# Where the modulation weights' dot products run beside three FFNs, and when a third FFN forms its sums of blocks

## The chip, the cores and the metric

The kernel runs on one core of a Trainium2 chip. The metric is the device time of one execution in microseconds (us); lower is better. PE is TensorE's matmul queue, DVE is VectorE, ACT is ScalarE, POOL is GpSimd, and SP is the queue from which nearly all transfers are issued.

## The reference, cut to what matters

Two layers run over 640 tokens: 128 context tokens and 512 latent tokens. Each layer has an FFN, a mixing of four head groups, and a second FFN. Each of these is normed, modulated and gated by vectors computed from the condition:

```
mod = silu(cond) @ w_mod + b_mod            # 9 vectors of 1024 for each layer and each condition
sh1, sc1, g1, sh2, sc2, g2, sh3, sc3, g3 = split(mod, 9)
x = x + 0.5 * g1 * swiglu(modulate(rmsnorm(x, nw0), sh1, sc1), w_in0, w_out0)
x = x + g2 * mixing(modulate(rmsnorm(x, nw1), sh2, sc2))
x = x + 0.5 * g3 * swiglu(modulate(rmsnorm(x, nw2), sh3, sc3), w_in1, w_out1)
swiglu(h) = (silu(h @ w_gate) * (h @ w_up)) @ w_out      # hidden width 2816
```

All of it is float32.

## The kernel before, in words

The activations lie transposed, 128 of the 1024 channels to a tile `x` and the 640 tokens in two groups of 320. A float32 product is done as three passes in a rounded format (fp32r): an operand is split into `hi`, a copy that ACT rounds, and `lo`, the difference that DVE takes (`split` and `wsplit`; the subtraction is line 61). So each weight tile of 128 x 1024 numbers goes from a load (`raw`, three buffers) to `hi` on ACT, to `lo` on DVE, and only then to PE; `hi` and `lo` have three buffers each.

Four FFNs run one after the other: the first (layer 0, function `ffn`), the second (layer 0 behind the mixing), the third (layer 1 before the mixing) and the fourth (layer 1 behind it); the last three are `ffn7`. The hidden width has 22 tiles. The first `ndir` of them (2, 12 and 2 in the second, third and fourth FFN) are direct: `direct` does for each token group the gate product and the up product, 24 matmuls each, so 96 in a tile, then `sg` (silu times up) and the split of the result into `gh` and `gl`. The other tiles are "quads" (`quad`): gate and up over both token groups as seven products of 12 matmuls in place of eight, as in Strassen's scheme. They need sums of weight blocks (`sa`, `sb`, made by DVE from `raw`) and sums of activation blocks (`T`, made by `sums(j)` from the normed values `nv` in `V`: four sums and three splits into `th` and `tl` for each j). A quad's products are taken in the order B21, B11, T3, T2, T4, then, between the products of the next quad, T1 and B22. After 5, 10, 15 and 19 tiles `down` multiplies by the output weights, eight column blocks, and adds to `x` with the gate (`accumulate`).

The modulation vectors of later norms are computed meanwhile on DVE. `modulation` is a generator: for each of 72 tiles of 128 outputs a layer it loads 128 x 1024 weights (`wm`, two buffers) and does two dot products with the condition (`modpiece`, the line 271, tile `wmj`), one for each condition; each call of `next` does one such piece. `some(rate)` adds a rate to a credit and calls `next` for each whole unit. The rates of an FFN are three: for each token group of a direct tile, for each column block of `down`, and for each quad. What is left is done before the last part. With `PIN`, a piece is pinned behind everything that was written before it on DVE.

For all the rest a planner sets each engine's order from what is written: it takes what is ready by its own costs, in the order of priority, and gives out buffers; an engine then does its instructions strictly in that order. So where a piece is written changes what the planner puts ahead of what.

Of the kernel before, what the change touches and what calls it, by code (L numbers as in the profile page):

```python
# [53 lines left out]
class Trunk:  # L54
# [486 lines left out]
    def ffn7(self, li, w, todo, ndir, rates, after_group):  # L541
        I, n = self.I, 2 * w
        pool = lambda name: self.tc.tile_pool(name=name, bufs=2, side="right", reuse_waits="tile")
        with pool("ws") as sp, pool("ffn") as mp, pool("mods") as modp, self.tmp():
            mods = self.modulation(todo, modp, bufs=MBUF, pin=PIN) if todo else iter(())
            self.G = []
            credit = [0.0]

            def some(rate):

                credit[0] += rate
                while credit[0] >= 1.0:
                    next(mods, None)
                    credit[0] -= 1.0

            def finish(q):
                for _ in q:
                    pass

            def down(ff, nk):  # L560

                G, self.G = self.G[:nk], self.G[nk:]
                for m in range(8):
                    hi, lo = self.wload(I["ffnoutA"][li, w, m, :, ff * 128 : (ff + nk) * 128], nk * 128)
                    for g in range(2):
                        ps = self.mmp.tile([128, 512], F32, tag="mm", name="mm")[:, :320]
                        self.mm3(ps, [(hi[:, k * 128 : (k + 1) * 128], lo[:, k * 128 : (k + 1) * 128]) + G[k][g]
                                      for k in range(nk)])
                        self.accumulate(li, n, m, g, ps)
                    some(rates[1])  # L570

            def direct(f):

                ws = [self.wload(I["ffnin"][li, w, 2 * f + i], 1024) for i in range(2)]
                sg = mp.tile([128, 640], F32, tag="sg", name="sg", bufs=2)
                gh = self.ring("gh", 640, F32R)
                gl = self.ring("gl", 640, F32R)
                for g in range(2):
                    c = slice(320 * g, 320 * g + 320)
                    self.act(sg[:, c], self.unit(ws[0], g, shifts=False), AF.Silu)  # L580
                    self.tt(sg[:, c], self.unit(ws[1], g, shifts=False), sg[:, c], MUL)
                    self.split(gh[:, c], gl[:, c], sg[:, c])
                    some(rates[0])
                self.G.append([(gh[:, 320 * g : 320 * g + 320], gl[:, 320 * g : 320 * g + 320]) for g in range(2)])

            ends = [sum(FFN_CHUNKS[: i + 1]) for i in range(len(FFN_CHUNKS))]
            for f in range(ndir):
                direct(f)
                if f < 2:
                    self.sums(f)  # L590
                if f + 1 in ends:
                    nk = FFN_CHUNKS[ends.index(f + 1)]
                    down(f + 1 - nk, nk)
            for j in range(2):
                self.split(self.hw[0][1][:, 2 * j : 2 * j + 2, 0:320], self.hw[1][1][:, 2 * j : 2 * j + 2, 0:320], self.V[0][j])
            prev = None
            for f in range(ndir, 22):
                q = self.quad(li, w, f, sp, mp, f == 21)
                next(q)
                if prev is not None:  # L600
                    next(prev)
                next(q)
                if prev is not None:
                    finish(prev)
                    if f in ends:
                        ci = ends.index(f)
                        down(f - FFN_CHUNKS[ci], FFN_CHUNKS[ci])
                prev = q
                some(rates[2])
            finish(prev)  # L610
            for _ in mods:
                pass
            nk = FFN_CHUNKS[-1]
            ws = [self.wload(I["ffnoutB"][li, w, b], 1024) for b in range(3)]
            G = self.G
            for g in range(2):
                for m in range(8):
                    if g and m == NPOS:
                        next(done, None)
                    ps = self.mmp.tile([128, 512], F32, tag="mm", name="mm")[:, :320]  # L620
                    parts = []
                    for k in range(nk):
                        b, j = divmod(m * nk + k, 8)
                        parts.append((ws[b][0][:, j * 128 : (j + 1) * 128],
                                      ws[b][1][:, j * 128 : (j + 1) * 128]) + G[k][g])
                    self.mm3(ps, parts)
                    self.accumulate(li, n, m, g, ps)
                    if li + 1 < NL or w == 0:
                        self.square(m, g)
                if g:  # L630
                    next(done, None)
                done = after_group(g)
                next(done, None)
            next(done, None)
# [777 lines left out]
    def run(self):  # L1412
        self.setup()
        with self.tc.tile_pool(name="start", bufs=2, side="right", reuse_waits="tile") as p, self.tmp():
            nc = self.nc
            cb = self.condb_start(p)
            self.xload(self.I["xT"])
            norms = [self.norm(0, 0, g, nc.vector, True) for g in range(2)]
            scale = self.modulation([(0, 1)], p, tiles=range(4, 8), bufs=SMB, cb=cb)
            shift = self.modulation([(0, 0)], p, tiles=range(2 * SPE, 8), bufs=SMB, cb=cb)  # L1420
            for j in range(2 + SPE):
                self.modulation_start(0, 1 if j < 2 else 0, p, range(j % 2, j % 2 + 1) if j < 4 else range(j - 2, j - 1))
                for gen in (scale, scale) if j < 2 else (shift,):
                    next(gen, None)
                for g in range(2):
                    if j == SORD[g] or j == SORD[2 + g]:
                        next(norms[g], None)
            for _ in shift:
                pass
            self.shifts(0, 0)  # L1430
            ahead = [self.wload(self.I["ffnin"][0, 0, i], 1024) for i in range(2)]
            for n in norms:
                next(n, None)
        kern = self.filters(range(NL))
        todo = [[(0, i) for i in range(2, 9)], [(1, 0), (1, 1)],
                [(1, i) for i in range(2, 8)], [(1, 8)]]
        for li in range(NL):
            def n1(g):
                if g == 0:
                    self.shifts(li, 1)  # L1440
                yield from self.norm(li, 1, g)
                self.xspill(li, g)

            def n2(g):
                yield from self.norm7(li, 2, g)

            def n3(g):
                if li + 1 < NL:
                    yield from self.norm7(li + 1, 0, g)
                else:  # L1450
                    self.store(g)
                    yield

            if li == 0:
                self.ffn(li, 0, todo[0], RATES[0], n1, ahead)
            else:
                self.ffn7(li, 0, todo[2], NDIR[1], RATES[2], n1)
                self.fac.close()
            for m in range(8):
                for g in range(2):  # L1460
                    self.tap(f"x1_{li}_{m}_{g}", self.x[m][g])
            self.mix(li, kern, n2)
            for m in range(8):
                for g in range(2):
                    self.tap(f"x2_{li}_{m}_{g}", self.x[m][g])
            self.ffn7(li, 1, todo[2 * li + 1], NDIR[2 * li], RATES[2 * li + 1], n3)
        self.fac.close()
# [12 lines left out]
CGACT = True  # L1480
MBUF = 2
NPOS = 8
RATES = 2.0, (1.5, 1.0, 0.5), (2.2, 1.0, 1.0), (2.0, 1.0, 3.0)
PIN = True
WB = 3
EACT = 1
# [164 lines left out]
```

## Time and profile before

| | us |
|---|---|
| median of three runs | 2776.7 (2774.94 to 2779.11) |
| the profiled execution | 2773.57 |
| its span, first to last instruction | 2771.8 |
| PE busy in the span | 2671.7 (96%) |
| DVE busy | 1959.7 (71%) |
| ACT busy | 1030.2 (37%) |

Busy PE time is modelled at its end, since matmuls are pipelined: the start of one to the start of the next is the better measure of its pace. Of the chain of work that ended last, 89% is PE's and 5% DVE's. The second FFN begins at about 997 us of the span, the third at 1445, the fourth at 2324.

### The profile page before, as it was taken

The numbers are of one execution on the slowest core, as the hardware profiler recorded it, in microseconds if no ns is written. First come the engines' busy times: TensorE is split into PE (matmuls) and PEld (weight loads), VectorE is DVE, ScalarE is ACT, GpSimd is POOL, SyncE is SP. The second block draws the span as 40 slices with busy tenths as digits, with TensorE's granted clock in tenths as the row PEclk, the third lists the DMA queues.
The fourth block names the chain that finished last, engine by engine and source line by source line (L and its number), as shares of the span: only waits on it lengthen the run. The fifth ranks groups of instructions, "written<-read, shape, count | busy, mean of one in ns | idle before, by whom it ended". The sixth has DMA issues, their size and how long they took to land.

```text
span 2771.8 us, 45385 instructions
## 1 busy us (share of the span) xinstructions
PE 2671.7 (96%) x17870; PEld 2575.6 (93%) x17870; DVE 1959.7 (71%) x4050; ACT 1030.2 (37%) x2042; POOL 114.0 (4%) x191
## 2 busy tenths in 40 slices
PE   5999999999999989999999999998999998999999
PEld 3889999989999979999988999998999997999999
DVE  5886666665685687776667777787658578876666
ACT  3222222242455353433353223334335535343342
POOL 0000000020010020000020000002001002000000
PEclk9999999999999999999999999999999999999999
DMA  7435444431221323333213443334212132322222
GB/s 247 145 125 197 142 135 148 137 103 66 81 78 42 108 69 107 105 111 121 84 61 118 158 149 129 117 130 148 85 57 96 36 106 68 107 79 82 85 69 91
DMA packets 118389, 299.64 MB, mean 108 GB/s; under 512 B 19747, under 2 KB 42483, under 8 KB 117664
## 3 DMA queue, kind: packets, MB, share of 16 engines
q1 hardware_dynamic: 118176, 296.74, 32.6%
q8 instruction: 141, 2.31, 0.3%
q14 instruction: 72, 0.59, 0.1%
HBM read 282.49 MB, written 14.20 MB: 107 GB/s over the span
## 4 chain that ended last, share of the span: by engine, by line
PE 89%; DVE 5%; issue 2%; POOL 1%; ACT 1%; DMA 1%; SPq 0%; POOLq 0%; DVEq 0%; ACTq 0%
PE mm L88 68%; PE mx L88 10%; PE mc L88 6%; PE mb L88 3%; PE mx L93 2%; DVE lo L61 1%; POOL nsum L287 1%; DVE x L70 1%; DVE wmj L271 1%; ACT hi L76 0%; POOL nrs L120 0%; DVE hl L61 0%; DVE tl L61 0%; DVE nv L61 0%; DVE gl L61 0%
## 5 line engine op out<-in xcount | busy, mean ns | idle before, releaser
L88 PE MATMUL mm<-hh,lo 128*128 128x320 f32 (+2 forms) x2936 | 922.8, 315 | 13.0 <-DVE lo L61 13.0
L88 PE MATMUL mm<-hh,hi 128*128 128x320 f32 (+2 forms) x2936 | 927.6, 317 | 6.8 <-ACT hh L76 4.1
L88 PE MATMUL mm<-hl,hi 128*128 128x320 f32 (+2 forms) x2936 | 924.3, 315 | 2.5 <-DVE hl L61 2.1
L76 ACT CAST hi<-raw 128x1024 fp32r<-128x1024 f32 (+3 forms) x390 | 338.5, 868 | 779.0 <-PE mm L88 704.4
L88 PEld LDWEIGHTS mm<-hh,lo 128*128 128x128 f32 (+1 forms) x2936 | 558.8, 190 | 20.3 <-DVE lo L61 14.1
L88 PEld LDWEIGHTS mm<-hh,hi 128*128 128x128 f32 (+1 forms) x2936 | 557.1, 190 | 15.0 <-ACT hh L76 5.7
L88 PEld LDWEIGHTS mm<-hl,hi 128*128 128x128 f32 (+1 forms) x2936 | 556.9, 190 | 12.8 <-issue 5.1
L61 DVE TENSOR_TENSOR lo<-raw,hi 128x1024 fp32r<-128x1024 f32 (+3 forms) x390 | 387.6, 994 | 175.0 <-ACT hi L76 172.9
L88 PE MATMUL mm<-gh,hi 128*128 128x320 f32 x1408 | 438.4, 312 | 5.5 <-DVE x L70 5.5
L88 PE MATMUL mm<-gl,hi 128*128 128x320 f32 x1408 | 436.3, 311 | 0.5 <-DVE gl L61 0.3
L88 PE MATMUL mm<-gh,lo 128*128 128x320 f32 x1408 | 434.5, 309 | 0.0
L70 DVE SCALAR_TENSOR_TENSOR x<-mm,gate,x 128x128 f32<-128x128 f32 (+2 forms) x576 | 234.4, 434 | 175.2 <-PE mm L88 172.7
L271 DVE CUSTOM_DVE_ANT_0 wmj<-wm,condb 128x1024 bf16<-128x1024 f32 x264 | 321.2, 1217 | 3.0 <-ACT condb L73 1.2
L88 PEld LDWEIGHTS mm<-gh,hi 128*128 128x128 f32 x1408 | 265.1, 188 | 11.0 <-PE mm L88 9.0
L88 PEld LDWEIGHTS mm<-gl,hi 128*128 128x128 f32 x1408 | 265.3, 188 | 3.9 <-issue 1.8
L88 PEld LDWEIGHTS mm<-gh,lo 128*128 128x128 f32 x1408 | 265.0, 188 | 0.3 <-issue 0.2
L88 PE MATMUL mc<-th,lo 128*128 128x320 f32 x400 | 123.4, 309 | 0.0
L88 PE MATMUL mc<-th,hi 128*128 128x320 f32 x400 | 123.3, 308 | 0.0
L88 PE MATMUL mc<-tl,hi 128*128 128x320 f32 x400 | 123.3, 308 | 0.0
L287 POOL TENSOR_TENSOR nsum<-nsum,nsq 128x320 f32<-128x320 f32 x60 | 54.8, 914 | 1350.6 <-ACT nsq L73 945.8
L76 ACT CAST gh<-sg 128x640 fp32r<-128x640 f32 (+1 forms) x85 | 51.6, 607 | 103.7 <-DVE sg L61 103.7
L70 DVE SCALAR_TENSOR_TENSOR gu<-mm,cg,sg 128x128 f32<-128x128 f32 (+2 forms) x66 | 27.2, 435 | 76.2 <-ACT cg L76 49.0
(283 smaller groups left out, 3500.6 us busy)
## 6 DMA issues: line engine op xcount, KB each, us to landing
raw<-in_ffnin SPq DMA_DIRECT2D x176, 512.0 KB, 3.5
wm<-in_wmodT SPq DMA_DIRECT2D x132, 512.0 KB, 3.5
raw<-in_ffnoutA SPq DMA_DIRECT2D x96, 320.0 KB, 2.8
raw<-in_mixin SPq DMA_DIRECT2D x52, 512.0 KB, 3.4
raw<-in_ffnoutA SPq DMA_DIRECT2D x32, 256.0 KB, 2.6
wms<-in_wmod SPq DMA_DIRECT2D x12, 512.0 KB, 3.4
raw<-in_ffnoutB SPq DMA_DIRECT2D x12, 512.0 KB, 3.4
raw<-in_mixout SPq DMA_DIRECT2D x16, 384.0 KB, 2.9
```

What stands on the lines that cost most here:

```text
L61: self.nc.vector.tensor_tensor(out, a, b, op=op)
L70: self.nc.vector.scalar_tensor_tensor(out, a, s, b, op0=op0, op1=op1)
L76: self.nc.scalar.copy(out, in_)
L88: return self.nc.tensor.matmul(out, lhsT=lhsT, rhs=rhs, start=start, stop=stop, **k)
L93: self.nc.tensor.transpose(out, in_, self.ident[b : b + n, b : b + n])
L271: return self.nc.vector.tensor_tensor_reduce(junk, raw, cb, 1.0, 0.0, op0=MUL, op1=ADD, accum_out=out)
L287: (adder or (self.nc.vector if g and m > 5 else self.nc.gpsimd)).tensor_tensor(s, s, sq, op=ADD)
```

## The change

Two lists of numbers and one rule are changed. `todo` gives the last modulation vector (layer 1, index 8) to the third FFN in place of the fourth, which has none left. `RATES` are 0 for the direct tiles of the second and the fourth FFN. In the third FFN (`ndir` of 12, so `late` is 3) the rates have four entries: 0 beside the first direct tile, after which the list is shortened to 3.2 for each token group of a direct tile (before: 2.2), 1.0 and 1.0. And there `sums(0)` and `sums(1)` are written after the fourth and the fifth direct tile, before after the first and the second.

```
             ends = [sum(FFN_CHUNKS[: i + 1]) for i in range(len(FFN_CHUNKS))]
+            late = 0 if ndir < 6 else 3
             for f in range(ndir):
+                if late and f == 1:
+                    rates = rates[1:]
                 direct(f)
-                if f < 2:
-                    self.sums(f)
+                if 0 <= f - late < 2:
+                    self.sums(f - late)
...
         todo = [[(0, i) for i in range(2, 9)], [(1, 0), (1, 1)],
-                [(1, i) for i in range(2, 8)], [(1, 8)]]
+                [(1, i) for i in range(2, 9)], []]
...
-RATES = 2.0, (1.5, 1.0, 0.5), (2.2, 1.0, 1.0), (2.0, 1.0, 3.0)
+RATES = 2.0, (0, 1.0, 0.5), (0, 3.2, 1.0, 1.0), (0, 0, 0)
```

The third FFN has 96 pieces before and 112 after, the fourth 16 before and none after, the second 32 in both.

DVE's order at the start of the third FFN before, from the end of the first direct tile's second token group on (`raw_15012` and `raw_15018` are the gate and the up weight of the second tile, `nv` and `tl` belong to the sums of blocks):

```order
L61 TENSOR_TENSOR gl_14876<-sg_14874,gh_14875 128x320
L271 ISA wmj_14997,mod1_108<-wm_14995,condb_14931 128x1024
L271 ISA mod1_108 128x1
L61 TENSOR_TENSOR nv_14832<-nv_14832,nv_14760 128x640
L271 ISA wmj_14999,mod1_108<-wm_14995,condb_14931 128x1024
L271 ISA mod1_108 128x1
L61 TENSOR_TENSOR tl_9460<-nv_14832,th_9459 128x2x320
L61 TENSOR_TENSOR mod1_108<-mod1_108,par1_93 128x2
L61 TENSOR_TENSOR nv_14782<-nv_14782,nv_14832 128x640
L61 TENSOR_TENSOR lo_15015<-raw_15012,hi_15014 128x1024
L61 TENSOR_TENSOR tl_9460<-nv_14782,th_9459 128x2x320
L61 TENSOR_TENSOR lo_15021<-raw_15018,hi_15020 128x1024
```

The same engine and place after, from the first `sg` of the first direct tile on (`raw_14985` and `raw_14991` are now the second tile's gate and up weight, `raw_15132` the third's gate weight):

```order
L61 TENSOR_TENSOR sg_14874<-mm_14903,sg_14874 128x320
L61 TENSOR_TENSOR lo_14988<-raw_14985,hi_14987 128x1024
L61 TENSOR_TENSOR hl1_106<-nv_14832,hh1_104 128x640
L61 TENSOR_TENSOR hl1_106<-nv_14839,hh1_104 128x640
L61 TENSOR_TENSOR gl_14876<-sg_14874,gh_14875 128x320
L61 TENSOR_TENSOR nv_14760<-nv_14818,nv_14760 128x640
L61 TENSOR_TENSOR nv_14771<-nv_14825,nv_14771 128x640
L61 TENSOR_TENSOR nv_14818<-nv_14818,nv_14832 128x640
L61 TENSOR_TENSOR lo_14994<-raw_14991,hi_14993 128x1024
L61 TENSOR_TENSOR sg_14874<-mm_14957,sg_14874 128x320
L61 TENSOR_TENSOR lo_15135<-raw_15132,hi_15134 128x1024
```

The second tile's gate `lo` moved from behind the second `gl` and its pieces to directly behind the first `sg`; the sums of blocks keep much of their early place.

DVE's order in the fourth FFN before, from the second direct tile's last `gl` to the first `lo` of the first quad (`raw_24312`):

```order
L61 TENSOR_TENSOR gl_24175<-sg_24173,gh_24174 128x320
L271 ISA wmj_24293,mod1_108<-wm_24291,condb_24080 128x1024
L271 ISA mod1_108 128x1
L61 TENSOR_TENSOR tl_23252<-nv_23991,th_23251 128x2x320
L271 ISA wmj_24295,mod1_108<-wm_24291,condb_24080 128x1024
L271 ISA mod1_108 128x1
L61 TENSOR_TENSOR nv_23945<-nv_23945,nv_23991 128x640
L61 TENSOR_TENSOR mod1_108<-mod1_108,par1_93 128x2
L61 TENSOR_TENSOR hl1_106<-nv_23912,hh1_104 128x640
L61 TENSOR_TENSOR hl1_106<-nv_23923,hh1_104 128x640
L61 TENSOR_TENSOR tl_23252<-nv_23945,th_23251 128x2x320
L61 TENSOR_TENSOR lo_24319<-raw_24312,hi_24318 128x1024
```

And after (`raw_24338` and `raw_24340` are the first quad's two weights, `sg_24213` is the second direct tile's, here its first token group):

```order
L61 TENSOR_TENSOR tl_23309<-nv_23991,th_23308 128x2x320
L61 TENSOR_TENSOR lo_24210<-raw_24207,hi_24209 128x1024
L61 TENSOR_TENSOR nv_24034<-nv_24034,nv_24048 128x640
L61 TENSOR_TENSOR lo_24345<-raw_24338,hi_24344 128x1024
L61 TENSOR_TENSOR tl_23309<-nv_24034,th_23308 128x2x320
L61 TENSOR_TENSOR nv_24048<-nv_24048,nv_23980 128x640
L61 TENSOR_TENSOR sa_24342<-raw_24340,raw_24338 128x512
L61 TENSOR_TENSOR sg_24213<-mm_24242,sg_24213 128x320
L61 TENSOR_TENSOR tl_23309<-nv_24048,th_23308 128x2x320
L61 TENSOR_TENSOR gl_24215<-sg_24213,gh_24214 128x320
L61 TENSOR_TENSOR nv_24002<-nv_24002,nv_24048 128x640
L61 TENSOR_TENSOR sb_24343<-raw_24340 128x512
```

The quad's first `lo` moved from behind the second tile to ahead of its first `sg`, and the quad's sums `sa` and `sb` begin there too. The second FFN is ordered in the same way.

SP's order in the third FFN where the quads begin, before (`raw_17269` and `raw_17271` are the first quad's weights, `raw_17371` and `raw_17373` the second's):

```order
L85 DMA raw_17269<-in_ffnin 128x1024
L85 DMA wm_17120<-in_wmodT 128x1024
L85 DMA raw_17271<-in_ffnin 128x1024
L85 DMA wm_17197<-in_wmodT 128x1024
L85 DMA raw_17371<-in_ffnin 128x1024
L85 DMA raw_17373<-in_ffnin 128x1024
L85 DMA wm_17258<-in_wmodT 128x1024
L85 DMA wm_17367<-in_wmodT 128x1024
L85 DMA raw_17505<-in_ffnin 128x1024
```

And after (the first quad's are `raw_17335` and `raw_17337`, the second's `raw_17437` and `raw_17439`, the third's first `raw_17572`):

```order
L85 DMA raw_17335<-in_ffnin 128x1024
L85 DMA raw_17337<-in_ffnin 128x1024
L85 DMA wm_17170<-in_wmodT 128x1024
L85 DMA raw_17437<-in_ffnin 128x1024
L85 DMA wm_17177<-in_wmodT 128x1024
L85 DMA raw_17439<-in_ffnin 128x1024
L85 DMA wm_17253<-in_wmodT 128x1024
L85 DMA wm_17261<-in_wmodT 128x1024
L85 DMA wm_17323<-in_wmodT 128x1024
L85 DMA wm_17433<-in_wmodT 128x1024
L85 DMA raw_17572<-in_ffnin 128x1024
```

Four loads of modulation weights now stand between the second quad's weights and the third's, where there were two. Late in the second mixing the planner also orders the retention part differently, though nothing is written differently there.

## Rows read from the trace of the kernel before

**Rows 1.** The page: span and instructions; busy time, share and instructions by engine.
```profile
span 2771.8 us, 45385 instructions
PE 2671.7 (96%) x17870; PEld 2575.6 (93%) x17870; DVE 1959.7 (71%) x4050; ACT 1030.2 (37%) x2042; POOL 114.0 (4%) x191
```
**Rows 2.** Waits of PE, whole span: waiter, awaited, us in total, times, longest.
```profile
PE mb L88 <- DVE lo L61: 14.4, 2, 8.4
PE mm L88 <- DVE lo L61: 13.0, 6, 6.8
```
**Rows 3.** PE's timeline, second FFN: start, us, instruction, count, idle before and its end.
```profile
1029.16 0.64 PE L88 MATMUL mb<-hh,lo 128*128 128x320 f32 x1 [6.01 <-DVE lo L61]
...
1032.21 0.31 PE L88 MATMUL mm<-hh,hi 128*128 128x320 f32 x1
```
**Rows 4.** PE's timeline, third FFN: first slow matmul and first fast one.
```profile
1471.05 0.64 PE L88 MATMUL mm<-hh,lo 128*128 128x320 f32 x1 [6.78 <-DVE lo L61]
...
1475.96 0.31 PE L88 MATMUL mm<-hh,lo 128*128 128x320 f32 x1
```
**Rows 5.** PE's timeline, fourth FFN: first slow matmul and first fast one.
```profile
2359.01 0.63 PE L88 MATMUL mb<-hh,lo 128*128 128x320 f32 x1 [8.39 <-DVE lo L61]
...
2363.41 0.31 PE L88 MATMUL mm<-hh,lo 128*128 128x320 f32 x1
```
**Rows 6.** Windows: stretch, us, busy by engine (count), granted clock, DMA share, GB/s.
```profile
1471.00:1475.70 4.70, 4.65 (x17) 4.65 (x18) 4.67 (x6) 0.19 (x1) 0.00 (x0) 0.50 0.59 204
```
**Rows 7.** DVE's timeline, second FFN, end of the direct tiles.
```profile
1022.59 0.49 DVE L61 TENSOR_TENSOR sg<-mm,sg 128x320 f32<-128x320 f32 x1 [0.22 <-PE mm L88]
...
1027.89 1.22 DVE L61 TENSOR_TENSOR lo<-raw,hi 128x1024 fp32r<-128x1024 f32 x1
```
**Rows 8.** DVE's timeline, third FFN, first direct tile.
```profile
1457.15 0.48 DVE L61 TENSOR_TENSOR sg<-mm,sg 128x320 f32<-128x320 f32 x1
...
1469.78 1.22 DVE L61 TENSOR_TENSOR lo<-raw,hi 128x1024 fp32r<-128x1024 f32 x1
1470.92 0.81 DVE L61 TENSOR_TENSOR tl<-nv,th 128x640 fp32r<-128x640 f32 x1
```
**Rows 9.** ACT's timeline, third FFN: the second tile's gate weight.
```profile
1442.31 1.03 ACT L76 CAST hi<-raw 128x1024 fp32r<-128x1024 f32 x1
```
**Rows 10.** DVE's groups by shape: the pieces (busy us, mean ns, idle before).
```profile
L271 DVE CUSTOM_DVE_ANT_0 wmj<-wm,condb 128x1024 bf16<-128x1024 f32 x264 | 321.2, 1217 | 3.0 <-ACT condb L73 1.2 <-DMA wm<-in_wmodT 0.5
```
**Rows 11.** DVE's timeline, third FFN: two pieces, and first `sg` of two tiles.
```profile
1481.42 1.22 DVE L271 CUSTOM_DVE_ANT_0 wmj<-wm,condb 128x1024 bf16<-128x1024 f32 x1
...
1482.68 1.23 DVE L271 CUSTOM_DVE_ANT_0 wmj<-wm,condb 128x1024 bf16<-128x1024 f32 x1
...
1494.02 0.49 DVE L61 TENSOR_TENSOR sg<-mm,sg 128x320 f32<-128x320 f32 x1 [1.97 <-PE mm L88]
...
1508.26 0.49 DVE L61 TENSOR_TENSOR sg<-mm,sg 128x320 f32<-128x320 f32 x1 [2.10 <-PE mm L88]
```
**Rows 12.** Windows: direct tiles of the third FFN, quads of the fourth.
```profile
1471.00:1542.00 71.00, 70.95 (x464) 70.95 (x465) 53.17 (x95) 17.48 (x29) 0.00 (x0) 0.97 0.44 138
2374.00:2405.00 31.00, 31.00 (x213) 31.00 (x212) 29.10 (x52) 14.74 (x25) 0.00 (x0) 1.00 0.32 101
```
**Rows 13.** DVE's timeline, third FFN, from the last direct tiles to the second quad's `lo`.
```profile
1679.01 0.69 DVE L61 TENSOR_TENSOR sa<-raw 128x512 f32<-128x512 f32 x1 [4.85 <-DMA raw<-in_ffnin]
...
1699.74 0.48 DVE L61 TENSOR_TENSOR sg<-mm,sg 128x320 f32<-128x320 f32 x1
1700.14 0.68 DVE L61 TENSOR_TENSOR sa<-raw 128x512 f32<-128x512 f32 x1
...
1705.13 1.21 DVE L61 TENSOR_TENSOR lo<-raw,hi 128x1024 fp32r<-128x1024 f32 x1
```
**Rows 14.** SP's timeline, third FFN: the load of the first quad's up weight.
```profile
1674.12 0.33 SPq L85 DMA_DIRECT2D raw<-in_ffnin  x1
```
**Rows 15.** Waits of PE in the second mixing's end (2195 to 2330).
```profile
PE mx L93 <- DVE y L61: 0.6, 1, 0.6
```

## The prediction

> **What bounds the kernel now.** I read first the shares of busy time: TensorE (PE) is busy 96% of a span of 2771.8 us [rows 1], so the change can win only in what PE stands still, and in what it runs below full speed. Next I read who PE waited for over the whole span. Two of its lines are of one kind: PE waits for `lo`, VectorE's (DVE's) part of splitting a weight into two float32r halves, 14.4 us in two waits and 13.0 us in six [rows 2]. Then PE's timeline around the longest of each: 6.01 us in the second FFN, where the first seven-product tile (a quad) begins [rows 3], 6.78 us in the third, where the second direct tile begins [rows 4], 8.39 us in the fourth, again at the first quad [rows 5]. Sum 21.18 us.
>
> PE also comes back slowly. From 1471.05 to 1475.96 it starts 18 matmuls, 0.267 us apart [rows 4], where the granted clock is 0.50, that is 1.2 of 2.4 GHz [rows 6], after standing still for 6.78 us. At full clock a direct tile of 96 matmuls takes 14.24 us, from the first `sg` of one tile to that of the next [rows 11], so 0.148 us each. The 18 lost 4.91 - 2.67 = 2.24 us. Likewise 11 in 3.05 us lost 1.42 us [rows 3], and 16 in 4.40 us lost 2.03 us [rows 5]. So the three places cost 21.18 + 5.69 = 26.9 us.
>
> Last I read DVE's own timeline there, to see that it is not idle but busy with other things: modulation pieces (`wmj`, 1.217 us each [rows 10]) written before that `lo`, and the sums of blocks. In the third FFN the second tile's gate weight had its `hi` half at 1442.31 [rows 9], but its `lo` begins at 1469.78, behind two half tiles' pieces [rows 8].
>
> **The change part by part.**
>
> *Third FFN, first tiles.* In the order after the change this `lo` stands directly behind the first `sg`, which begins at 1457.15 before [rows 8], with nothing of the modulation ahead; its `hi` is there. It takes 1.14 us from start to start of the next [rows 8] and ends by about 1459, 5 us before the first tile is through at 1464.27 (1471.05 - 6.78). The up weight's `lo` follows behind six more DVE instructions, none listed with over 0.82 us: by 1464, and PE needs it a quarter of a tile after 1464.27 (24 matmuls, 3.6 us). I take the whole 6.78 + 2.24 us as gained. The block sums, though written three tiles later, still start ahead of it in the planned order, since they need nothing but their inputs; I cost their move at nothing. Their cover is the 19 us of DVE time in the next ten direct tiles, below.
>
> *Second and fourth FFN, first quad.* Six and eight pieces leave the first two tiles. In the order after, the quad's first `lo` stands ahead of the second tile's first `sg`, not behind its last `gl`: by DVE's steps some 7 us before PE needs it. What is late next is the third product's weight (`lo` from `sa`): behind the last `sg` (1022.59 before [rows 7]) come `sg`, one `hl`, `gl`, one `sb` and this `lo`, 0.40 + 0.82 + 0.40 + 0.68 + 1.14 = 3.4 us (steps and listed times from [rows 8, 13]), so 1026.0. PE needs it after the 20 matmuls of the first two products that are left at the gap's start (1023.15): 1023.15 + 20 x 0.148 = 1026.1. It just fits; I allow 0.2 us in each FFN. Gained: 6.01 + 1.42 + 8.39 + 2.03 = 17.9, less 0.4.
>
> *Where the pieces go.* The second FFN has 32. Its `down` passes (8 at each of the first, 1 per column block) and its quads (0.5 each) take all of them before the last `down` ends, at the rates that they had. That cover is good: in the fourth FFN before, DVE was busy 29.1 of 31 us beside quads with pieces at rate 3, and PE 31.0 of 31 [rows 12]. I cost it at nothing; bounds -0.5 and +2 us (the condition loads and their ScalarE pass sit elsewhere in the queues). The fourth FFN has none now, and its 16 pieces, 19.5 us of DVE at 1.217, go to the third with its eight loads of 512 KB.
>
> *Third FFN, tiles two to twelve.* Pieces per tile go from 4.4 to 6.4. One costs 1.26 us from start to start [rows 11]. With two `lo` (2.3), four `sg`/`gl` (1.6) and three adds of the bias (0.3) a tile asks 8.1 + 4.2 = 12.3 of 14.24 us, where before it was 9.7: DVE's spare time falls from 4.5 to 1.9 us a tile, 19 us over ten. Before, DVE was busy 53.2 of 71 us there and PE never waited [rows 12]. So most tiles cost nothing, but one place has a debt. SP issues loads in order, and the up weight of the first quad waits for a buffer: it was issued at 1674.12 [rows 14], DVE stood 4.85 us for it, to 1679.01 [rows 13]. After the change it waits for the same buffer behind the same `lo`, so the stall stays, and then there are, up to the second quad's first `lo` and with it, 13 pieces (15.6 us), four wide `lo` (4.6), three `sa`, three `sb` and a narrow `lo` (4.8, at 0.68 [rows 13]), five `sg` and four `gl` (3.6, at 0.40 [rows 13]), two `hl` (1.6) and eight small ones (0.7): 30.9 us, or a us less where the listed times overlap, from 1679.0 to some 1709.5. PE needs it 60 matmuls after the tiles end at 1699.7: 1708.6. Before, it was ready at 1706.3 [rows 13]. It would be a us late; with some more for ScalarE's `hi` and the weight behind it I take 1.6 us of waiting in all at this join. Bounds: 0 (the order hides it) and 10 (each of ten tiles a us late).
>
> *The retention part of the second mixing* is ordered differently too, by the planner alone: fewer dense matmuls fill PE between small ones that wait for DVE. Before, this stretch had one such wait, 0.6 us [rows 15]. I take 0.5 us more, between -0.6 and +3.
>
> Sum: 26.9 - 0.4 - 1.6 - 0.5 = 24.4 us gained. The profiled execution took 2773.57 us (1.8 around its span): it would be 2749.2. The median of the runs is 2776.7, 3.1 us above; the same 24.4 from it is 2752.3. I predict **2752.5 us**. What cannot be told from no change here is 0.2%, 5.5 us.
>
> The restarts are the least certain of the terms that I count whole. Rows show 11, 18 and 16 slow matmuls after gaps of 6 to 8.4 us. The Trainium skill, TensorE: Matmul & The Clock Gate, section "What's actually happening", says that the number of slow ones varies between runs of one kernel and gives 6, 11 and 14 for one. At 0.119 us lost each that would be 2.1 to 5.0 us for the three as an estimate from that page, and a gain of 20.8 to 23.7 us in place of 24.4. The trace has 45 in all, above that.
>
> **Rivals.**
>
> A: *the third FFN takes a part back.* Three loads of modulation weights now follow each other in SP's queue ahead of a raw weight, and each waits for one of two buffers that DVE frees; the raw weight comes late, DVE stands as at 1674 [rows 13, 14], and with 1.9 us to spare a tile it reaches PE. For: that stall; against: no PE wait there before. If each of ten tiles loses 1 us on average: 10 less gained, 2752.5 + 10 - 1.6 = 2761. The skill's page TensorE: Matmul & The Clock Gate, section "Architectural detail", says that VectorE is a strict first-in first-out queue; the stall agrees.
>
> B: *the gaps stay in part.* The first `lo` comes early but PE then waits for the next ones in line (`lo` from `sa`, the up weight), whose inputs pass through ScalarE too. For: 0.2 us of margin above. If 3 us stay at each of three places, each short enough to leave the clock alone, 9 us less: 2761.5; if half of all stays, 13.5 less: 2766.
>
> C: *slower.* The same mechanism as A, but at every burst: at 3.2 modulation tiles a direct tile and two buffers, a piece of the next tile follows its freed buffer by less than a load takes to land (4.9 us from issue to the end of the stall [rows 13, 14]). Two such stalls a tile, 9.8 us less 1.9 spare, over eleven tiles is 87 us; the kernel gets slower from a loss of 2.4 us a tile, that is from 4.3 us of stall in each. One such stall in each (3.0 lost) gives 33 - 24 = 9 us slower, 2785. Against: with 2.2 such tiles a direct tile PE was busy for all of 71 us [rows 12].
>
> D: *it does nothing*: the planner's order counts little, since DVE's total work is unchanged and PE's waits only move. 2776. Against: DVE has 29% idle.
>
> **Chances.** Forecast (20 to 30 gained, 2747 to 2757) 0.60; A 0.15; B 0.12; C 0.05; D 0.05; and 0.03 for more than 30 gained, as when the fourth FFN also wins by the loads that it no longer has. The range 2746 to 2768 holds the forecast, A, B and most of the unknown costs' bounds. Faster by over 0.2%: 0.90, within: 0.05, slower: 0.05.
>
> **What would show it.** In the profile after: no wait of PE for `lo` over 2 us at the starts of the second, third and fourth FFN, and granted clock 1.00 there; `wmj` in none of the first two tiles of the second FFN, nowhere in the fourth; DVE near 86% busy in the third FFN's direct tiles with PE at its 14.24 us a tile; a wait of PE of 0.5 to 2 us at the third FFN's first or second quad. A would show as DVE waiting for raw or modulation loads there and PE for `lo`; B as PE waits of 2 to 4 us one product further on. The forecast is wrong if the third FFN from its second tile on is over 5 us longer than before, or the three gaps keep over a third of their 21 us.

## The result, and the profile after

Median 2748.3 us (2743.5 to 2752.3, four runs) against 2777.9 us for the kernel before (2774.9 to 2781.7, four runs); ratio 0.9892, 95% interval 0.9872 to 0.9912. The forecast was 2752.5 us, 2746 to 2768. The profiled executions took 2773.57 and 2748.34 us: 25.2 us less, where the sum of the prediction said 24.4.

The page of the kernel after, to be held against [rows 1], and the same line of PE's waits over the whole span as in [rows 2]:

```profile
span 2746.5 us, 45381 instructions
PE 2668.9 (97%) x17870; PEld 2572.8 (94%) x17870; DVE 1958.3 (71%) x4050; ACT 1028.3 (37%) x2041; POOL 114.2 (4%) x191
...
PE mm L88 <- DVE lo L61: 6.5, 6, 1.8
```

DVE does the same work, and PE stands still 77.6 us of its span where it stood 100.1: 22.5 us less. Its busy time is 2.8 us less. The line of `mb` behind `lo` (14.4 us before) is gone, and that of `mm` has fallen from 13.0 to 6.5 us: its wait of 6.8 is gone. DVE's timeline of the kernel after shows why, at the end of the second FFN's direct tiles (to [rows 7]), in the third FFN's first tile (to [rows 8]) and at the end of the fourth FFN's direct tiles:

```profile
1025.09 0.49 DVE L61 TENSOR_TENSOR sg<-mm,sg 128x320 f32<-128x320 f32 x1 [0.24 <-PE mm L88]
...
1027.23 1.22 DVE L61 TENSOR_TENSOR lo<-sa,hi 128x1024 fp32r<-128x1024 f32 x1
...
1455.58 0.48 DVE L61 TENSOR_TENSOR sg<-mm,sg 128x320 f32<-128x320 f32 x1
1455.98 1.22 DVE L61 TENSOR_TENSOR lo<-raw,hi 128x1024 fp32r<-128x1024 f32 x1
...
2335.89 0.49 DVE L61 TENSOR_TENSOR sg<-mm,sg 128x320 f32<-128x320 f32 x1 [0.25 <-PE mm L88]
...
2338.03 1.22 DVE L61 TENSOR_TENSOR lo<-sa,hi 128x1024 fp32r<-128x1024 f32 x1
```

No piece of modulation stands between; the fourth FFN has none at all, and the second FFN's first begins at 1050.7. In the third FFN that `lo` begins 0.4 us after the first `sg`, where it began 12.6 us after it. In the other two, even the third product's weight (`lo` from `sa`) starts 2.1 us after the tile's last `sg`, and PE does not wait there.

The windows of the kernel after (stretch, us, busy time of PE, PEld, DVE, ACT and POOL with counts, granted clock, DMA share, GB/s): around the three places, and the third FFN from the second direct tile on, to [rows 12]:

```profile
1010.00:1035.00 25.00, 25.00 (x171) 24.96 (x170) 23.84 (x35) 15.21 (x25) 0.00 (x0) 1.00 0.20 65
1452.00:1476.00 24.00, 24.00 (x165) 24.00 (x164) 22.72 (x35) 14.53 (x26) 0.00 (x0) 1.00 0.25 85
2325.00:2360.00 35.00, 35.00 (x238) 34.96 (x238) 31.17 (x45) 17.33 (x28) 0.00 (x0) 1.00 0.28 91
...
1457.00:1640.00 183.00, 183.00 (x1240) 183.00 (x1239) 155.91 (x300) 48.48 (x78) 0.00 (x0) 1.00 0.51 167
```

At the three places PE stands still nowhere, at full clock. DVE is busy for 85.2% of the third FFN's tiles, PE all the time, at full clock too.

### The profile page after: what moved, and what is told of

It reads as the page before. It is cut to its first block, busy times and chain, and to the rows that moved or that the text cites. A ratio compares the mean times of both kernels' runs of the same rounds, so it can differ in the third digit from the quotient of the medians.

```text
span 2746.5 us, 45381 instructions
## 1 busy us (share of the span) xinstructions
PE 2668.9 (97%) x17870; PEld 2572.8 (94%) x17870; DVE 1958.3 (71%) x4050; ACT 1028.3 (37%) x2041; POOL 114.2 (4%) x191
## 4 chain that ended last, share of the span: by engine, by line
PE 91%; DVE 4%; issue 2%; POOL 2%; ACT 1%; DMA 1%; SPq 0%; POOLq 0%; ACTq 0%; DVEq 0%
PE mm L88 69%; PE mx L88 10%; PE mc L88 6%; PE mb L88 3%; PE mx L93 2%; DVE lo L61 1%; POOL nsum L287 1%; DVE x L70 1%; POOL nrs L120 0%; ACT hi L76 0%; DVE hl L61 0%; DMA condrow<-in_condr 0%; DVE nsum L287 0%; POOL arr L120 0%; DVE ndg L61 0%
```

## The experiments

In the table are stage lengths in us, each from the first of the ten matmuls of a norm's sum (`mx<-ones,nsum`) to that of the next stage's norm, so that they add up; the last ends with the span. Mixing 1 and what lies before it (977 to 980 us) is left out. The stages are those of the one profiled execution; the median, in the last column, is that of all executions of the kernel.

```
kernel     2nd FFN  3rd FFN  mixing 2  4th FFN   median
before       452.1    476.3    398.6    467.5    2777.9
after        445.3    468.5    397.4    456.1    2748.3
e1_24        444.9    488.6    404.5    456.9    2778.3
e2_third     452.4    471.7    396.9    466.9    2768.3
e3_sums      445.5    468.8    397.5    456.3    2749.5
e4_last      447.7    472.1    396.4    467.6    2763.8
e5_24b       445.4    478.3    397.9    456.2    2758.0
e6_heavy     445.6    488.1    397.1    456.2    2769.0
e7_half      449.6    465.1    395.7    467.4    2766.3
e8_quads     444.9    469.9    399.0    456.2    2756.6
e9_28        445.7    478.7    397.6    459.3    2760.7
e10_38       445.5    473.9    399.7    456.9    2752.2
e11_after    445.3    468.9    397.6    456.2    2748.0
```

**Two of the three places (e1_24).** The kernel before, edited:

```
-RATES = 2.0, (1.5, 1.0, 0.5), (2.2, 1.0, 1.0), (2.0, 1.0, 3.0)
+RATES = 2.0, (0, 1.0, 0.5), (2.2, 1.0, 1.0), (0, 0, 0)
...
-                [(1, i) for i in range(2, 8)], [(1, 8)]]
+                [(1, i) for i in range(2, 9)], []]
```

> Kernel before, with pieces taken from beside the first tiles of the second and the fourth FFN only; the third FFN keeps its 2.2 from the first tile on and its early sums, and takes the last part in. My theory (each gap is its own, made by the pieces that stand ahead of the quad's first lo): 6.01 + 1.42 and 8.39 + 2.03 less 0.4 go, 17.5 us; from the median of 2777.9 to 2760.4; PE's wait of 6.8 us for lo at the third FFN's second tile stays, the two waits of mb for lo are gone. Rival R1 (the gain comes from the third FFN's new order, the sums' move included): 2770 or more. Rival R2 (work that leaves the fourth FFN comes back as waiting in the third, which was full): the sixteen pieces cost up to 19.5 us there, 2770 to 2780, with new PE waits at the third's quads.

2778.3 us, ratio 0.9998 (0.9990 to 1.0007): nothing gained. The table shows both halves of it: the second and the fourth FFN give 7.2 and 10.6 us, as the theory had it, and the third FFN with the mixing behind it takes 18.2 back. The time fits the rivals R1 and R2; the place is not R2's: PE's timeline of e1_24 (start, us, instruction, idle before and its end) has its new waits in the third FFN's last down and behind it, not at its quads, and the window there shows the clock.

```profile
1893.63 0.39 PE L88 MATMUL mm<-gh,hi 128*128 128x320 f32 x1 [0.65 <-DVE sc L70]
1896.98 0.46 PE L88 MATMUL mm<-gh,hi 128*128 128x320 f32 x1 [1.80 <-DVE mod L61]
1900.33 0.61 PE L88 MATMUL mm<-gh,hi 128*128 128x320 f32 x1 [0.75 <-DVE mod L61]
...
1935.94 0.64 PE L88 MATMUL mm<-hh,lo 128*128 128x322 f32 x1 [5.10 <-DVE lo L61]
...
1896.00:1911.00 15.00, 11.01 (x37) 9.55 (x38) 14.77 (x33) 2.13 (x5) 5.32 (x4) 0.54 0.61 186
```

What is left of the list when the quads are through is issued there in one go. At a rate of 2.2, 24 x 2.2 + 42 (two downs beside direct tiles 16, ten quads 10, two downs beside quads 16) = 94.8 of 112 pieces are through by then, and 17 are left. Most of them stand between the last down's adds to `x`, where DVE is busy 14.77 of 15 us. PE stops at nearly every block, and the granted clock is 0.54. (`mod` is only the DVE instruction that ended last; what PE can need there is the add to `x` ahead of it.) The last five pieces begin between 1914.0 and 1922.3, beside the norm of mixing 2, and PE's wait of 5.10 us at 1935.94 stands behind it: of the 18.2 us, 12.3 are in the third FFN and 5.9 in mixing 2.

**The same with nothing left over (e5_24b).** e1_24 with 3.1 from the third FFN's second tile on:

```
-RATES = 2.0, (0, 1.0, 0.5), (2.2, 1.0, 1.0), (0, 0, 0)
+RATES = 2.0, (0, 1.0, 0.5), (2.2, 3.1, 1.0, 1.0), (0, 0, 0)
...
             for f in range(ndir):
+                if ndir > 5 and f == 1:
+                    rates = rates[1:]
                 direct(f)
```

> Kernel before, with no pieces beside the first tiles of the second and the fourth FFN, the last part in the third FFN, and there 2.2 pieces per half tile beside the first tile, as before, and 3.1 from the second on (4.4 + 68.2 + 42 beside downs and quads = 114.6, so that all 112 are through before the last down; the kernel of e1_24 got 52.8 + 42 = 94.8 through, and 17 were left for the last down). My theory after e1_24 (the two gaps went there too, but the 17 left over cost PE as much at the third FFN's end): with nothing left over the 17.5 us show, 2778.0 - 17.5 = 2760.5, with the 6.8 us wait at the third FFN's second tile as it was and no wait for modulation at its end. Rival R2 (the third FFN has no room for sixteen more pieces, wherever they stand): 2770 to 2778 again.

2758.0 us, 18.2 us less than before on the same chip (ratio 0.9934, 0.9921 to 0.9946), and PE's one wait over 3 us from the second FFN on is the one that was left in:

```profile
1467.83 0.64 PE L88 MATMUL mm<-hh,lo 128*128 128x320 f32 x1 [6.77 <-DVE lo L61]
```

R2 falls: the third FFN has room for sixteen more pieces, as long as they are through in time. R1 falls with it, since here the third FFN's first tile and its sums are as before.

**How much may be left over (e9_28).** The kernel after, edited:

```
-RATES = 2.0, (0, 1.0, 0.5), (0, 3.2, 1.0, 1.0), (0, 0, 0)
+RATES = 2.0, (0, 1.0, 0.5), (0, 2.8, 1.0, 1.0), (0, 0, 0)
```

> Kernel after, with 2.8 pieces per half tile in place of 3.2 in the third FFN from its second tile on: 61.6 + 42 = 103.6 of 112 are through before the last down, 8 are left over for it. My theory (what is left over is exposed there nearly whole: 17 left over cost some 18 us in e1_24): 8 x 1.0 to 1.2 less what the last down has to spare, 4 to 9 us slower than after, with short waits of PE for DVE in the last down and a low granted clock there. Rival R8 (the third FFN's rate doesn't matter below 3.2, the loss in e1_24 was another): within 2 us of after.

2760.7 us, 12.7 more than the kernel after on the same chip (e11_after): more than the 4 to 9 expected. PE's waits of e9_28 in the last down (1876 to 1900: awaited, us in total, times, longest), its window there, two neighbouring pieces of DVE, and an addition on POOL:

```profile
PE mm L88 <- DVE mod L61: 5.9, 5, 2.0
...
1880.00:1900.00 20.00, 14.02 (x59) 12.60 (x60) 17.63 (x40) 5.74 (x12) 8.17 (x7) 0.70 0.58 175
...
1882.09 1.22 DVE L271 CUSTOM_DVE_ANT_0 wmj<-wm,condb 128x1024 bf16<-128x1024 f32 x1
...
1883.49 1.62 DVE L271 CUSTOM_DVE_ANT_0 wmj<-wm,condb 128x1024 bf16<-128x1024 f32 x1
...
1882.68 1.35 POOL L287 TENSOR_TENSOR nsum<-nsum,nsq 128x320 f32<-128x320 f32 x1 [442.28 <-ACT nsq L73]
```

The waits are 5.9 us. Some 30 matmuls at half clock, 0.119 us each, make 3.6 more. Some pieces there took 1.62 us for 1.22. In the profile the third FFN is 10.2 us longer than after, about the time of eight pieces. Another 3.2 us are in the fourth FFN, which has no pieces: in its first 40 us the granted clock is 0.83 here and 0.96 after, and whether the pieces left over bring that about isn't shown. The rate 3.2 of the change is what just empties the list, 22 x 3.2 + 42 = 112.4. R8 is out.

**The third FFN alone (e2_third).** The kernel before with the three lines for `f == 1` of e5_24b, and

```
-RATES = 2.0, (1.5, 1.0, 0.5), (2.2, 1.0, 1.0), (2.0, 1.0, 3.0)
+RATES = 2.0, (1.5, 1.0, 0.5), (0, 2.2, 1.0, 1.0), (2.0, 1.0, 3.0)
```

> Kernel before, with no pieces beside the third FFN's first tile and 2.2 from its second on; sums written early as before, second and fourth FFN as before. My theory: the gap of 6.78 us and its slow restart of 2.24 us go, 9.0 us: 2768.9; the two mb waits of 6.0 and 8.4 us stay. Rival R3 (the early sums must move too, since they stand ahead of the second tile's lo): 3 us or more of that wait stay, 2772 to 2778.

2768.3 us (ratio 0.9961, 0.9948 to 0.9973): 9.7 less than before. The wait at the second tile is gone, so R3 falls: the sums need not move. Of the 9 us the profile has only 4.6 in the third FFN itself: 22 x 2.2 + 42 = 90.4 of 96 pieces are through, 5.6 are left over, and the window 1880 to 1900 has its clock at 0.83. The profiled execution is 6.6 us shorter than that of the kernel before, 1.7 of it in mixing 2; where the rest of the medians' 9.7 lies is not shown.

**The sums (e3_sums).** The kernel after, edited:

```
-                if 0 <= f - late < 2:
-                    self.sums(f - late)
+                if f < 2:
+                    self.sums(f)
```

> Kernel after, with the third FFN's sums of blocks written behind its first two tiles again. My theory (as in the prediction, their move is worth nothing, since the planner lets them go where DVE is free): the time of after, 2748.3, within 3 us, and no wait for lo over 2 us. Rival R3 (the sums stand ahead of the second tile's lo when written early): 3 to 9 us slower, 2751 to 2757, with that wait back.

2749.5 us (2746.4 to 2750.6), 1.2 more than after, within the runs' spread; no wait for `lo` over 1.8 us. Their move is worth nothing that can be measured.

**The last part (e4_last).** The kernel after, edited:

```
-RATES = 2.0, (0, 1.0, 0.5), (0, 3.2, 1.0, 1.0), (0, 0, 0)
+RATES = 2.0, (0, 1.0, 0.5), (0, 2.2, 1.0, 1.0), (0, 1.0, 6.0)
...
-                [(1, i) for i in range(2, 9)], []]
+                [(1, i) for i in range(2, 8)], [(1, 8)]]
```

> Kernel after, with the last part of the modulation kept in the fourth FFN: none beside its two direct tiles, 6 pieces per quad (16 must be through before its first down, and only three quads stand ahead of that); the third FFN at 2.2 from its second tile. My theory (the fourth's quads have little room: DVE was busy 29.1 of 31 us there at 3 pieces a quad [rows 12], about 0.8 us to spare a quad of 12.4 us): three more pieces a quad, 3.8 us, less 0.8, over 2.7 quads, are 8 us of DVE that PE waits for in part: 5 to 9 us slower than after, 2753 to 2757, with PE waiting for lo at the fourth's second or third quad. Rival R4 (moving the last part to the third FFN is worth nothing, it is enough to keep the first tiles free): 2748, within 2 us.

2763.8 us, 15.5 more than after, against 5 to 9 expected. The fourth FFN takes 11.5 us back, all of the 11.4 that it had gained. PE's timeline of e4_last, in the second quad:

```profile
2369.60 0.63 PE L88 MATMUL mc<-th,hi 128*128 128x320 f32 x1 [4.08 <-ACT hi L76]
...
2374.23 0.64 PE L88 MATMUL mc<-th,lo 128*128 128x320 f32 x1 [2.53 <-DVE lo L61]
```

These 6.6 us and some 20 matmuls at half clock behind them, 2.4 us, are 9.0. A further 3.6 us are in the third FFN, which at 2.2 has 5.6 pieces left over, as in e2_third. R4 falls: with the sixteen pieces at six a quad, the one way that was tried, keeping the fourth FFN's first tiles free gains nothing there.

**Half the pieces (e7_half).** The kernel before with the lines for `f == 1`, and

```
-RATES = 2.0, (1.5, 1.0, 0.5), (2.2, 1.0, 1.0), (2.0, 1.0, 3.0)
+RATES = 2.0, (0.75, 1.0, 0.5), (1.1, 2.5, 1.0, 1.0), (2.0, 1.0, 3.0)
```

> Kernel before, with half the pieces ahead of the gap in two places: 0.75 in place of 1.5 per half tile beside the second FFN's two direct tiles (3 pieces for 6), 1.1 in place of 2.2 beside the third FFN's first tile (2 for 4), then 2.5 so that all are through; the fourth FFN as before. My theory (each piece that stands ahead of that lo costs its 1.26 us): the gap in the second FFN 6.0 - 3 x 1.26 = 2.2 us, in the third 6.8 - 2 x 1.26 = 4.3; time 2778 - 3.8 - 2.5 = 2771.7, or down to 2768 if PE comes back at full clock from the shorter gaps. Rival R6 (the planner moves that lo as a whole, so a gap is there whole or not at all): 6.0 and 6.8, or 0 in one of them.

2766.3 us, 10 less than before (ratio 0.9952, 0.9936 to 0.9968). The profiled execution is the shortest of six, 2756.4, so that its stages in the table are shorter than those of the median. In the third FFN neither number holds: two pieces for four leave no wait at all. DVE's timeline of e7_half beside the first tile, and PE's at the second FFN's first quad:

```profile
1456.97 1.22 DVE L271 CUSTOM_DVE_ANT_0 wmj<-wm,condb 128x1024 bf16<-128x1024 f32 x1
...
1458.85 1.22 DVE L61 TENSOR_TENSOR lo<-raw,hi 128x1024 fp32r<-128x1024 f32 x1
1459.99 0.49 DVE L61 TENSOR_TENSOR sg<-mm,sg 128x320 f32<-128x320 f32 x1
...
1028.83 0.63 PE L88 MATMUL mc<-th,hi 128*128 128x320 f32 x1 [2.75 <-ACT hi L76]
```

With one piece a half tile the planner set the `lo` ahead of the second `sg`; with two, behind four pieces. That is R6. In the second FFN the first product's `lo` was in time and PE waited at the third product, 2.75 us (near the theory's 2.2, but not at its place), for an `hi` that waits for `sb` and `sa` behind the three pieces.

**More than DVE can take (e6_heavy).** The kernel after, edited:

```
-RATES = 2.0, (0, 1.0, 0.5), (0, 3.2, 1.0, 1.0), (0, 0, 0)
+RATES = 2.0, (0, 1.0, 0.5), (0, 5.0, 1.0, 1.0), (0, 0, 0)
```

> Kernel after, with 5.0 pieces per half tile in place of 3.2 in the third FFN from its second tile on. A tile then asks 10 x 1.26 + 4.2 = 16.8 us of DVE for 14.24 of PE, for the 9.6 tiles that the pieces last (16 go beside downs). My theory (DVE's budget a tile decides, and 3.2 stands 1.9 us under it): 2.56 us late a tile, 24.6 in all, less some 4 that the first lo is ahead and the 4.35 us a down that DVE waits: 10 to 22 us slower than after, 2758 to 2770, in many PE waits for lo of 1 to 3 us in the direct tiles. Rival R5 (the planner keeps PE's needs first and lets pieces slip): within 3 us of after, 2746 to 2751. Rival A of the prediction, stronger (the modulation loads hold the raw weights back in SP's queue): over 22 us slower, over 2770, with DVE waiting for raw loads.

2769.0 us, 20.7 more than after, in the forecast's range. The window 1457 to 1640, as above, and the two largest groups of PE's waits from 1457 to 1700 (awaited, us in total, times, longest):

```profile
1457.00:1640.00 183.00, 173.73 (x1153) 171.62 (x1151) 168.13 (x334) 45.22 (x73) 0.00 (x0) 0.99 0.58 188
...
PE mm L88 <- DVE mod L61: 4.7, 4, 1.8
PE mm L88 <- DVE lo L61: 4.2, 4, 1.4
```

From 1457 to 1700 PE waits 14.1 us in all, in five such groups, and some 52 matmuls at half clock add 6.2. The waits do not stand in the tiles, where they were expected, but at the joins between tiles and downs. Stalls of DVE for loads grow too (13 for modulation weights, 7.7 us in all), less than rival A asked.

**A little under what DVE can take (e10_38).** The kernel after, edited:

```
-RATES = 2.0, (0, 1.0, 0.5), (0, 3.2, 1.0, 1.0), (0, 0, 0)
+RATES = 2.0, (0, 1.0, 0.5), (0, 3.8, 1.0, 1.0), (0, 0, 0)
```

> Kernel after, with 3.8 pieces per half tile in place of 3.2: 7.6 x 1.26 + 4.2 = 13.8 of 14.24 us of DVE a tile, and all pieces are through two tiles sooner. My theory (DVE's budget a tile decides): within 3 us of after, no PE wait over 1 us in the direct tiles. Rival A (no room to spare: a raw load that comes late is not made up any more, as in e6_heavy at the joins to the downs): 4 to 12 us slower, with PE waits at the two downs between the direct tiles.

2752.2 us (2751.0 to 2756.9), 4.2 more than e11_after (2745.6 to 2748.5): little more than the kernel after has between its own runs, where the longest took 2752.3. The profiled execution is the longest of the four. In it the tiles hold, with DVE busy 166.40 of 183 us, and one wait over 1 us appears, at the third FFN's join from direct tiles to quads, not at the downs that rival A had named:

```profile
1457.00:1640.00 183.00, 182.94 (x1236) 182.41 (x1236) 166.40 (x326) 48.95 (x78) 0.00 (x0) 1.00 0.56 181
...
1704.94 0.41 PE L88 MATMUL mc<-th,hi 128*128 128x320 f32 x1 [2.23 <-ACT hi L76]
...
1707.04 0.47 PE L88 MATMUL mc<-tl,hi 128*128 128x320 f32 x1
1707.31 0.47 PE L88 MATMUL mc<-th,lo 128*128 128x320 f32 x1
```

This is the join at which the prediction had expected 1.6 us at 3.2, though at another product, the second quad's third. SP issues a raw weight at 1697.23, behind four modulation loads that it began at 1681.77, and the `sa` that leads to this `hi` begins at 1700.97, 3.7 us later; such a load lands after 3.4 us in the median. That fits rival A's mechanism. But DVE stands idle nowhere between 1690 and 1704.9, and pieces run ahead of that `sa` and behind it (1699.43 and 1701.97), so DVE's own work may have held the `hi` as well as the load; no run takes the one or the other away.

**The pieces spread into the quads (e8_quads).** The kernel after, edited:

```
-RATES = 2.0, (0, 1.0, 0.5), (0, 3.2, 1.0, 1.0), (0, 0, 0)
+RATES = 2.0, (0, 1.0, 0.5), (0, 2.2, 1.0, 3.2), (0, 0, 0)
```

> Kernel after, with the same 112 pieces of the third FFN spread otherwise: 2.2 per half tile (for 3.2) in the direct tiles and 3.2 per quad (for 1) in its ten quads: 48.4 + 32 + 32 beside downs = 112.4. My theory (what counts is that none stands ahead of a first tile's lo, that none is left for the last down, and that no stretch asks DVE for more than PE takes; quads of the fourth FFN took 3 at 29.1 of 31 us [rows 12], 3.2 ask 0.25 us more of the 0.76 to spare): the time of after, 2748 to 2751. Rival R7 (the quads' chain of sa, sb, lo does not bear that many pieces between): one to two us late in each of ten quads, 2755 to 2768.

2756.6 us (2750.5 to 2760.8), 8.3 more than after; the profiled execution is the shortest of the six, 2750.5. It shows one wait of 2.5 us at the last down, and of R7's lateness, one to two us in each quad, only waits for `lo` of 0.5 us and less. So the time is R7's and its place is not shown; where the other five executions lose 4 to 10 us more stays open. Their mean granted clock is 0.989 to 0.991 against 0.993.

**The kernel after once more (e11_after),** without an edit.

> Kernel after, unchanged, for comparison on the same chip: 2748, within 4 us. If the spread between its runs is of the clock after short stops (as my theory of the restarts has it), the longer runs show the lower mean granted clock, about 2.7 us for each 0.001; if it is of something else (loads, say), clock and time go apart.

2748.0 us (2745.6 to 2748.5), with clock and time in step: 0.993 in the shortest of four, 0.991 in the two longest.

## Why the prediction was right, point by point

*The three gaps.* Right, each at its forecast size: 21.2 us of standstill are gone. e1_24 and e5_24b take two of them away and get 17.8 and 18.0 us in the second and fourth FFN (forecast 17.5); e2_third takes away the third's wait.

*The slow restarts.* At the three places the clock is at 1.00, as said. But PE's busy time, which holds the slow matmuls, fell by 2.8 us, where this term was 5.69. Part of it came back at another place, the norm ahead of the third FFN (it begins at 1429.4 before and at 1424.6 after). Windows there before, and then after:

```profile
1430.00:1440.00 10.00, 9.20 (x60) 8.49 (x59) 7.58 (x20) 7.09 (x18) 4.78 (x5) 1.00 0.00 0
1440.00:1450.00 10.00, 7.18 (x34) 5.38 (x33) 8.73 (x18) 6.41 (x15) 4.22 (x2) 0.76 0.16 54
```
```profile
1430.00:1440.00 10.00, 9.36 (x52) 9.10 (x50) 6.90 (x17) 8.42 (x19) 4.23 (x4) 0.81 0.00 0
1440.00:1450.00 10.00, 7.55 (x33) 5.93 (x34) 8.94 (x19) 4.98 (x11) 2.82 (x1) 0.71 0.26 93
```

In the timelines, some 19 matmuls run at half clock around that norm before and some 36 after: 17 x 0.119 = 2.0 us. Among the other profiles e5_24b and e11_after have some 37 each, e1_24 and e8_quads some 18, though all four have the second FFN of the kernel after; so the number at this norm does not go with the change. This term was sized right for its places, but the net depends on how many other restarts an execution has; it was the term called least certain. The Trainium skill (TensorE: Matmul & The Clock Gate, section "What's actually happening") states that the number of slow ones varies between runs of one kernel; the traces agree. Its counts of 6, 11 and 14 are another kernel's; here 9 came after 2.75 us in e7_half and 11, 18 and 16 at the three places [rows 3 to 5].

*The third product's weight, -0.4.* Not needed. The steps were right (3.3 us from `sg` to the start of what follows that `lo`, forecast 3.4), and it comes in time in both FFNs.

*The third FFN's tiles.* DVE at 85.2% where 86% was forecast, PE at its pace. The wait at the join, -1.6, did not come: PE's waits from 1625 to 1760 sum to 0.6 us. DVE's timeline after has the end of its stall and the second quad's first `lo`, and PE's has the first quad's first matmul and the one that needs this `lo`:

```profile
1666.48 0.69 DVE L61 TENSOR_TENSOR sa<-raw 128x512 f32<-128x512 f32 x1 [3.60 <-DMA raw<-in_ffnin]
...
1696.02 1.22 DVE L61 TENSOR_TENSOR lo<-raw,hi 128x1024 fp32r<-128x1024 f32 x1
...
1688.34 0.32 PE L88 MATMUL mb<-hh,hi 128*128 128x320 f32 x1
...
1697.47 0.31 PE L88 MATMUL mb<-hh,lo 128*128 128x320 f32 x1
```

DVE's work from the stall to the end of that `lo` was right: 30.9 us forecast, 30.8 measured (to 1697.24), with the 13 pieces. What the prediction had wrong is when the stall ends: it is 3.60 us where it was 4.85 [rows 13], and it ends 21.9 us before PE's first quad, where the prediction took 20.7. So the `lo` is there 0.2 us before PE needs it. A wait at this join came in e10_38's profiled execution, 2.23 us and a slow restart, at a rate one fifth higher.

*The second FFN's pieces in its downs and quads: 0.* Right: 445.3 us with them, 6.8 less than before.

*The retention part, -0.5.* Not there: one wait of 0.7 us for `y`, as before [rows 15].

*The block sums: nothing.* Right (e3_sums).

*What it left out.* The sum came out at 24.4 for the span's 25.3, in part by luck, since errors cancel: 2.9 us too much for restarts, 2.5 us of waits that did not come, and 1.3 us of other waits that fell. A bigger omission cost nothing by luck: the prediction took the rate 3.2 and the part's move as they were and named no price for pieces left over at the end of the list. e1_24 shows 18.2 us for 17 pieces, e9_28 12.7 us for 8 (10.2 of them in the third FFN), and the third FFNs of e2_third and e4_last 3.2 and 3.6 us for 5.6.

## What to carry to other kernels

Where a filler is spread beside the main work, look first for what it stands ahead of at a change of stage: here eighteen pieces of 1.2 us, on an engine that idles 29% of the time, lay in front of three operands and cost 27 us. Then count whether the filler is through at its last stop, since what is left over there is paid by waits and by the clock: here 17 pieces cost 18 us, eight 10 to 13, and between five and six some 3.5. Between these two ends there is an interval of rates that no busy share shows: 3.2 lies in it, 2.8 (12.7 us slower) and 5.0 (20.7 us slower) lie outside, and 3.8 (4.2 us slower) is at its edge. It comes from the count of pieces and from each stage's time per piece.

## What the runs showed of the hardware that was not expected

The spread within one kernel goes with the mean granted clock: e7_half's six runs go from 2756.4 us at 0.990 to 2768.1 us at 0.986. In e10_38, after a wait of 2.23 us, PE's first matmuls are fast, and those at half clock begin 2.1 us behind it, at 1707.04; after the three long waits of the kernel before, and after 2.75 us in e7_half, they are slow from the first on [rows 3 to 5]. Pieces of modulation took 1.62 us instead of 1.22 when they stood beside the last down (e9_28 at 1883.49), alternating with normal ones. In the thirteen traces, 14 of 3432 pieces are such, and each of the 14 begins while POOL runs an addition for the norm's sum (in e9_28 that from 1882.68 to 1884.03, above); of the others one does. That goes together each time, but no run takes the additions away to show that they are the cause.
